# Rope queries of a latent-attention head in a zero-padded slot of 128 rows

## Chip, cores and metric

The kernel runs on one core of a Trainium2 chip, in one launch. The metric is the device time of the core in microseconds (us). Everything is float32: products that need accuracy split a float32 operand into a high part (`fp32r`, the form that TensorE takes in one pass) and a low part (the rest, again `fp32r`), and add three products: high by high, high by low, low by high.

## What is computed

Two layers over 256 latent tokens and 256 context tokens of width 2048. The first layer has eight heads of neighbourhood attention and eight heads of multi-head latent attention; the second is a bidirectional gated DeltaNet. The change is in the latent attention of the first layer. Cut to that:

```python
def mla_latent_attention(qn, qr, kn, kr, v, kn_c, kr_c, v_c):
    def attend(args):
        qn_i, qr_i = args
        s_lat = (einsum('bhqd,bhkd->bhqk', qn_i, kn) + einsum('bhqd,bkd->bhqk', qr_i, kr)) * MLA_SCALE
        s_ctx = (einsum('bhqd,bhkd->bhqk', qn_i, kn_c) + einsum('bhqd,bkd->bhqk', qr_i, kr_c)) * MLA_SCALE
        p_lat, p_ctx = joint_softmax(s_lat, s_ctx, v.dtype)
        return einsum('bhqk,bhkd->bhqd', p_lat, v) + einsum('bhqk,bhkd->bhqd', p_ctx, v_c)
```

A score is thus the sum of a product over the 128 plain dimensions of a head (`qn`, `kn`) and of a product over its 64 rope dimensions (`qr`, `kr`); the rope key `kr` is the same for all heads.

## The kernel before

Everything lies feature-major: a tile has 128 features on its partitions (rows) and 512 tokens along it, 256 latent then 256 context. TensorE takes the sum over the rows.

**Queues.** Each engine works through its own queue in order. A scheduler lays these queues out when the program is built, from its own estimates of how long things take, so an instruction that is added on one engine can move others, far behind it as well. Loads are issued by the SP queue.

**First layer, neighbourhood heads** (lines 395 to 404). `na_head` makes three tiles of 128x512 with 48 products each and `attend` (lines 350 to 388) does the attention. The last of them, head 7, is made at line 443 and attended at line 455, after the preparation of the latent heads.

**Preparation of the latent heads** (lines 408 to 460). `craw` holds the two normed low-rank inputs; lines 449 to 451 scale them and split them into `ch`, high by a cast on ScalarE (line 450), low by a subtraction on VectorE (line 451). `ch` takes the buffer that `hh` had, and `qr`, the rope queries, that of `hl`; both can be written only when the last product of head 7 has read `hh` and `hl`. Lines 457 to 460 make the rope queries: `qr` comes from four tiles, each the product of a 512-wide weight slice with `ch`, and each holds two heads, one in rows 0 to 63, the other in rows 64 to 127. `roped` (lines 427 to 439) scales a tile, rotates its latent half with a permutation product (`pp`, line 434) and three VectorE instructions, and calls `both`, which writes the high part (ScalarE) and the low part (VectorE) into `qr`. The rope key `kr` (line 441) holds its 64 rows twice, in rows 0 to 63 and in rows 64 to 127.

**The eight latent heads** (lines 461 to 470). Each loads its weights, makes `qT`, `kT` and `vT` with 12 products each (`dense`, lines 85 to 93) and calls `attend`. `attend` has four blocks of queries per head (two of latent tokens with 512 keys, two of context tokens with 256). For each block, `product` (lines 346 to 348) adds three products of `qT` with `kT` over 128 rows into the score tile `sp`, and line 368 three more of `qr` with `kr` over the 64 rows of the head:

```python
r = slice(64 * (h % 2), 64 * (h % 2) + 64)
attend(*o, 8 + h, None, ([qr[r, 4 * i + h // 2] for i in range(2)], [kr[r, i] for i in range(2)]))
```

Then come the maximum (line 372), the exponential (line 375), the division, four transposes (`pt`, line 381), the split into `PT` (`both`), and the products with the values (`po`, line 386). There are two score tiles, so a block's products can start when the block two before has been read by the exponential.

**Beside it** (`later`, `adaln`, lines 107 to 145). The modulation vectors of the second layer are made in the gaps: loads of 512 KB from `dn_wm` into three buffers `mraw`, four products `pmod` with 32 output rows on each (line 127), and per 16 loads a copy and four transposes. The three buffers lie in a pool that is opened when `craw` is released (line 453). `pmod` stands in TensorE's queue among the products of the heads.

After the latent heads come the output projection of the first layer (lines 477 to 503) and the second layer, whose first part has VectorE at work nearly all the time (solving the triangular systems, lines 759 to 782) and many switches of ScalarE's function tables (`ACT_TABLE_LOAD`).

Of the kernel before, what the change touches and what calls it, by code (L numbers as in the profile page):

```python
# [10 lines left out]
AF = mybir.ActivationFunctionType  # L11
# [7 lines left out]
T = 512  # L19
EPS = 1e-6  # L20
NA_SCALE = 128 ** -0.5
MLA_SCALE = 192 ** -0.5
# [4 lines left out]
def trunk_kernel(ctx: ExitStack, tc: tile.TileContext, g):  # L27
    nc = tc.nc
    V, A, PE, P = nc.vector, nc.scalar, nc.tensor, nc.gpsimd
# [8 lines left out]
    def mm_tile():  # L38
        return mmp.tile([128, T], F32, name="mm", tag="mm")
# [4 lines left out]
    def cst(name, shape, src=None):  # L44
        t = const.tile(shape, F32, name=name, tag=name)
        if src is not None:
            nc.scalar.dma_start(t, src)
        return t
# [3 lines left out]
    ones = cst("ones", [128, 128])  # L52
# [190 lines left out]
    with tc.tile_pool(name="s0", bufs=2) as tp, tc.tile_pool(name="s0p", bufs=1, space=PSUM) as ps:  # L243
# [37 lines left out]
        for j, (k0, n) in enumerate(GROUPS):  # L281
            ahead = mods_of(j + 1) if j < end else iter(())
            for i in range(0, NS, 2):
                own = i < NP
                p = [pz[i + e] if own else mm_tile() for e in range(2)]
# [16 lines left out]
    with tc.tile_pool(name="ab", bufs=2, reuse_waits="tile") as tp, \  # L302
# [4 lines left out]
        def later(pool, parts, after=None):  # L307
            for l, chunks, lanes in parts:
                if lanes:
                    yield from adaln_lanes(l, ps, "pm", pool, chunks, after)  # L310
                else:
                    yield from adaln(l, ps, ("pm", "pm"), pool, [(4 * ch, 4) for ch in chunks], after=after)
# [3 lines left out]
        def unit(xh, xl, src=None):  # L316
            nonlocal u, last_mm
            if src is None:
                src = wab[u]
                u += 1  # L320
            p = mm_tile()
            for c in range(0, 2048, 1024):
                last_mm = dense(p, load_split(src[:, c:c + 1024], 1024), 0, 8, xh, xl, k0=c // 128, first=c == 0, last=c > 0)
                steps(ahead, pace)
            return p

        for j in range(NS, KT):
            p = unit(hh, hl)
# [3 lines left out]
        def parts(src, name, n=T, scale=1.0, pool=None, bufs=1):  # L332

            t = (pool or tp).tile([128, 2, n], F32R, name=name, tag=name, bufs=bufs)
            both(t[:, 0], t[:, 1], src, scale)
            return t

        def both(hi, lo, src, scale=1.0):
            if scale == 1.0:
                A.copy(hi, src)  # L340
                V.tensor_tensor(lo, src, hi.bitcast(F32), op=ALU.subtract)
            else:
                A.mul(hi, src, scale)
                V.scalar_tensor_tensor(lo, src, scale, hi.bitcast(F32), op0=ALU.mult, op1=ALU.subtract)

        def product(ps, a, b, first, last):
            for i, (x, y) in enumerate(((0, 0), (0, 1), (1, 0))):
                PE.matmul(ps, a(x), b(y), start=first and i == 0, stop=last and i == 2)  # L348

        def attend(qT, kT, vT, h, bias=None, rope=None):  # L350

            pv = ps.tile([128, 4, 128], F32, name="pv", tag="tr", bufs=TR)
            for b in range(4):
                PE.transpose(pv[:, b], vT[:, b * 128:(b + 1) * 128], ident)
            vt = parts(pv.rearrange("p b d -> p (b d)"), "vt")
            po = ps.tile([128, T], F32, name="po", tag="st", bufs=1)
            for s in range(2):
                nk = 4 if s == 0 else 2
                c0 = 0 if s == 0 else S
                N = nk * 128  # L360
                PT = tp.tile([128, 2, 4, S], F32R, name="PT", tag="PT", bufs=1)
                for qb in range(2):
                    q0 = s * S + qb * 128
                    sp = ps.tile([128, T], F32, name="sp", tag="sp")
                    product(sp[:, :N], lambda i: qT[:, i, q0:q0 + 128], lambda i: kT[:, i, c0:T], True, rope is None)
                    if rope is not None:
                        qr, kr = rope
                        product(sp[:, :N], lambda i: qr[i][:, q0:q0 + 128], lambda i: kr[i][:, c0:T], False, True)
                    if s == 0 and bias is not None:
                        V.tensor_tensor(sp[:, :S], sp[:, :S], bias[:, qb], op=ALU.add)  # L370
                    mx = tp.tile([128, 1], F32, name="mx", tag="mx")
                    V.tensor_reduce(mx, sp[:, :N], axis=AX.X, op=ALU.max, negate=True)
                    pr = tp.tile([128, T], F32, name="pr", tag="pr")
                    sm = tp.tile([128, 1], F32, name="sm", tag="sm")
                    A.activation(pr[:, :N], sp[:, :N], AF.Exp, bias=mx, accum_out=sm)
                    rc = tp.tile([128, 1], F32, name="rc", tag="rc")
                    V.reciprocal(rc, sm)
                    V.tensor_scalar(pr[:, :N], pr[:, :N], rc, None, op0=ALU.mult)
                    pt = ps.tile([128, 4, 128], F32, name="pt", tag="tr", bufs=TR)
                    for b in range(nk):  # L380
                        PE.transpose(pt[:, b], pr[:, b * 128:(b + 1) * 128], ident)
                    qs = slice(qb * 128, (qb + 1) * 128)
                    both(PT[:, 0, :nk, qs], PT[:, 1, :nk, qs], pt[:, :nk])
                for b in range(nk):
                    c = (b if s == 0 else 2 + b) * 128
                    product(po[:, s * S:(s + 1) * S], lambda i: vt[:, i, c:c + 128], lambda i: PT[:, i, b],
                            b == 0, b == nk - 1)
                V.tensor_tensor(go[s][:, h], po[:, s * S:(s + 1) * S], go[s][:, h], op=ALU.mult)
# [6 lines left out]
        def na_head(h):  # L395
            bias = tp.tile([128, 2, S], F32, name="bias", tag="bias")
            nc.sync.dma_start(bias, g["rpb"][h])
            qT = parts(unit(hh, hl), "qT", scale=NA_SCALE)
            kT = parts(unit(hh, hl), "kT")
            vT = keep(unit(hh, hl), "vT")  # L400
            return qT, kT, vT, h, bias
# [20 lines left out]
        krp = unit(hh, hl)  # L422
# [1 line left out]
        nc.scalar.dma_start(rt, g["ropet"])  # L424
        cosT, sinT, perm = rt[:, :S], rt[:, S:2 * S], rt[:, 2 * S:]

        def roped(p, hi, lo, scale):
            out = tp.tile([128, T], F32, name="rope", tag="rope", bufs=1)
            if scale == 1.0:
                A.copy(out, p)  # L430
            else:
                A.mul(out, p, scale)
            pp = ps.tile([128, S], F32, name="pp", tag="tr", bufs=TR)
            PE.matmul(pp, perm, out[:, :S], start=True, stop=True)
            t = tp.tile([128, S], F32, name="rtmp", tag="mtmp")
            V.tensor_tensor(t, pp, sinT, op=ALU.mult)
            V.tensor_tensor(out[:, :S], out[:, :S], cosT, op=ALU.mult)
            V.tensor_tensor(out[:, :S], out[:, :S], t, op=ALU.add)
            both(hi, lo, out)

        kr = tp.tile([128, 2, T], F32R, name="kr", tag="kr", bufs=1)
        roped(krp, kr[:, 0], kr[:, 1], 1.0)
        na7 = na_head(7)
        ch = big.tile([128, KT, T], F32R, name="ch", tag="hh")
        qr = big.tile([128, KT, T], F32R, name="qr", tag="hl")
        for i, gain in enumerate((q_gain, kv_gain)):
            for k in range(4):
                j = 4 * i + k
# [3 lines left out]
        cr.release()  # L452
        mr = tc.alloc_tile_pool(name="mr2", bufs=2, reuse_waits="tile")
        ahead = later(mr, ((1, (2, 3, 8), 0),))
        attend(*na7)
        w = load_split(g["ab_wqr"])
        for j in range(4):
            p = mm_tile()
            dense(p, w, j * 512, 4, ch, ch[:, 8:])
            roped(p, qr[:, j], qr[:, 4 + j], MLA_SCALE)  # L460
        for h in range(8):
            w = load_split(g["ab_wb"][h], 1536)
            o = []
            for j, (k0, name, sc) in enumerate(((0, "qT", MLA_SCALE), (4, "kT", 1.0), (4, "vT", 1.0))):
                p = mm_tile()
                last_mm = dense(p, w, j * 512, 4, ch, ch[:, 8:], k0)
                o.append(keep(p, name) if name == "vT" else parts(p, name, scale=sc))
            r = slice(64 * (h % 2), 64 * (h % 2) + 64)
            steps(ahead, 1)
            attend(*o, 8 + h, None, ([qr[r, 4 * i + h // 2] for i in range(2)], [kr[r, i] for i in range(2)]))  # L470

        steps(ahead)
        steps(later(mr, ((1, (9,), 0),), last_mm))
# [10 lines left out]
        for j in range(KT):  # L484
# [3 lines left out]
            p = unit(gh, gl, g["ab_wo"][j])  # L488
# [127 lines left out]
    with tc.tile_pool(name="dn", bufs=2, reuse_waits="tile") as tp, \  # L616
# [14 lines left out]
        p = dunit(U_BA, FULL)  # L631
# [4 lines left out]
        hi = slice(64, 128)  # L636
# [22 lines left out]
        for d in range(2):  # L659
# [4 lines left out]
            for h in range(2):  # L664
                a = (d + h) % 2
                r = slice(64 * h, 64 * h + 64)
# [503 lines left out]
        for st in range(-2, 64 + LAG):  # L1170
            i, n = st // 4, st % 4
            j, m = (st - LAG) // 4, (st - LAG) % 4
# [85 lines left out]
        i = 0  # L1258
        for u in [v for e in range(KT - NE) for v in (e, NE + e)]:
            k0 = 24 if u < NE else 0  # L1260
            w = load_split(g["dn_wo"][u][:, 128 * k0:], 4096 - 128 * k0)
            p = (mm_tile() if i % 2 else ps.tile([128, T], F32, name="mm2", tag="ks"))[:, :S]
# [120 lines left out]
```

## Time and profile before

| | |
|---|---|
| median of 3 runs | 2562.46 us (2559.86 to 2563.72) |
| the profiled execution | 2556.45 us, of which 2554.6 us are the span from the first to the last instruction |
| mean granted TensorE clock | 0.984; 1.00 in all windows from 320 to 1068 us |
| busy: TensorE, weight loads, VectorE, ScalarE | 2461.1, 2004.0, 1849.1, 1130.7 us |
| latent heads | about 731 to 885 us of the span |
| preparation of the latent heads | about 640 to 731 us |
| second layer, VectorE part | about 1140 to 1760 us |

In the profile PE is TensorE's products, PEld its weight loads, DVE VectorE, ACT ScalarE, POOL GpSimd; SPq is SyncE's queue, which issues loads. A row of the timeline gives the start and the length in us, the line, the operation, output and input tiles, the part of the array that a product takes (rows * columns, 128*128 or 64*128 or 128*32), the size of the moving input, how many instructions of the kind follow one another, and in brackets the idle time of the engine before it with what ended it. A product's length overlaps with that of the next one, so the cost of a product in a row of products is read from start to start.

### The profile page before, as it was taken

To read this page: it belongs to the slowest core of one execution; us is meant where nothing else is said; L and a number is where in the kernel's file an instruction comes from. 1 tells how busy PE (TensorE), PEld (TensorE's weight loads), DVE (VectorE), ACT (ScalarE), POOL (GpSimd) and SP (SyncE) were. 2 spreads that over 40 slices of the span, in tenths; PEclk is the share of its full clock that TensorE was granted. 3 is DMA by queue.
4 is the path that set the end of the run, shared out by engine and by line. 5 is a ranking of instruction groups with operands and counts; after the bars stand their busy time and mean duration, and the time that the engine had idled before them with its cause. 6 is when DMAs were issued, how large, how long until landed. Compare 5 with 4: busy or idle time off the path is not lost.

```text
span 2554.6 us, 43393 instructions
## 1 busy us (share of the span) xinstructions
PE 2461.1 (96%) x16586; PEld 2004.0 (78%) x16586; DVE 1849.1 (72%) x3543; ACT 1130.7 (44%) x2454; POOL 275.4 (11%) x261
## 2 busy tenths in 40 slices
PE   6999999999999999989998999998999999999998
PEld 4657888888767688758888988887777777778898
DVE  4544788873445688758999999996677777777654
ACT  4223323332334422378656655643444445445453
POOL 0000000000000000023223332300000000003000
PEclk9999999999999999999999999998999999999999
DMA  8872655532343367644554545573233333335454
GB/s 259 289 254 87 201 167 165 184 118 94 100 155 119 109 212 228 219 138 150 167 158 156 161 153 162 162 223 95 88 105 112 113 100 107 112 92 180 151 189 139
DMA packets 201808, 394.30 MB, mean 154 GB/s; under 512 B 68224, under 2 KB 109696, under 8 KB 201472
## 3 DMA queue, kind: packets, MB, share of 16 engines
q1 hardware_dynamic: 200448, 389.98, 48.7%
q8 instruction: 131, 2.15, 0.4%
q10 hardware_dynamic: 1152, 1.54, 0.2%
q14 instruction: 77, 0.63, 0.1%
HBM read 356.28 MB, written 35.13 MB: 153 GB/s over the span
## 4 chain that ended last, share of the span: by engine, by line
PE 76%; DVE 11%; issue 6%; DMA 3%; ACT 3%; SPq 0%; POOL 0%; DVEq 0%; POOLq 0%; ACTq 0%
PE mm L90 19%; PE mm L91 18%; PE mm L92 18%; PE pks L988 3%; PE pmod L127 3%; DVE wlo L78 2%; PE sp L348 2%; PE ptr L1000 2%; DVE acc L561 2%; PE po L348 1%; DVE outer L773 1%; PE ptr L1033 1%; DVE L L759 1%; DVE X L775 1%; DVE U L782 1%
## 5 line engine op out<-in xcount | busy, mean ns | idle before, releaser
L90 PE MATMUL mm<-hh,whi 128*128 128x512 f32 (+1 forms) x2784 | 986.4, 355 | 2.7 <-ACT t L638 2.2
L92 PE MATMUL mm<-hh,wlo 128*128 128x512 f32 (+1 forms) x2784 | 957.9, 344 | 7.3 <-DVE wlo L78 6.7
L91 PE MATMUL mm<-hl,whi 128*128 128x512 f32 (+1 forms) x2784 | 960.3, 345 | 0.4 <-issue 0.4
L77 ACT CAST whi<-raw 128x1024 fp32r<-128x1024 f32 (+2 forms) x346 | 338.3, 982 | 651.5 <-PE mm L91 495.5
L90 PEld LDWEIGHTS mm<-hh,whi 128*128 128x128 f32 x2784 | 533.7, 192 | 113.1 <-issue 32.0
L92 PEld LDWEIGHTS mm<-hh,wlo 128*128 128x128 f32 x2784 | 533.4, 192 | 71.7 <-DVE wlo L78 8.0
L91 PEld LDWEIGHTS mm<-hl,whi 128*128 128x128 f32 x2784 | 534.1, 192 | 63.0 <-issue 10.3
L78 DVE TENSOR_TENSOR wlo<-raw,whi 128x1024 fp32r<-128x1024 f32 (+2 forms) x346 | 403.8, 1169 | 200.4 <-ACT whi L77 198.5
L163 DVE SCALAR_TENSOR_TENSOR lacc<-mraw,cond,lacc 128x512 f32<-128x512 f32 x300 | 208.0, 742 | 0.0
L561 DVE SCALAR_TENSOR_TENSOR acc<-cin,taps,acc 128x508 f32<-128x508 f32 (+3 forms) x256 | 193.9, 758 | 6.7 <-ACT acc L552 4.3
L1010 DVE SCALAR_TENSOR_TENSOR vl<-ptr,egm,vh 128x128 fp32r<-128x128 f32 x224 | 64.7, 346 | 99.8 <-ACT rf L1007 39.5
L715 POOL TENSOR_TENSOR rhs<-ghl,incl 128x512 fp32r<-128x512 f32 (+1 forms) x96 | 113.8, 1199 | 190.4 <-PE pd L717 171.0
L773 DVE SCALAR_TENSOR_TENSOR outer<-L,bv,X 128x31 f32<-128x31 f32 (+15 forms) x248 | 116.7, 471 | 5.5
L127 PE MATMUL pmod<-mraw,cond 128*32 128x512 f32 (+2 forms) x640 | 93.7, 500 | 25.4 <-DMA mraw<-ab_wm 18.0
L1094 DVE TENSOR_TENSOR wlo<-raw,whi 128x1024 fp32r<-128x1024 f32 x84 | 102.4, 1219 | 14.1 <-ACT whi L1086 14.0
L194 POOL TENSOR_TENSOR rs<-ms,half 128x4 f32<-128x4 f32 (+1 forms) x5 | 4.7, 947 | 984.7 <-DVE ms L192 984.7
L575 ACT ACTIVATE ac<-acc 128x128 f32<-128x128 f32 x160 | 37.6, 302 | 151.2 <-DVE acc L561 151.2
L775 DVE TENSOR_TENSOR X<-X,outer 128x31 f32<-128x31 f32 (+15 forms) x248 | 98.7, 398 | 4.7
L90 PE MATMUL mm<-gh,whi 128*128 128x512 f32 x256 | 99.9, 391 | 1.7 <-DVE x1B L493 1.7
L91 PE MATMUL mm<-gl,whi 128*128 128x512 f32 x256 | 99.9, 390 | 0.2 <-DVE gl L481 0.2
L92 PE MATMUL mm<-gh,wlo 128*128 128x512 f32 x256 | 99.7, 389 | 0.0
L1004 ACT ACTIVATE vh<-ptr,egm 128x128 fp32r<-128x128 f32 x224 | 71.7, 377 | 60.8 <-PE ptr L1000 54.4
(289 smaller groups left out, 3557.7 us busy)
## 6 DMA issues: line engine op xcount, KB each, us to landing
raw<-dn_w SPq DMA_DIRECT2D x194, 512.0 KB, 4.1
mraw<-dn_wm SPq DMA_DIRECT2D x96, 512.0 KB, 4.7
mraw<-ab_wm SPq DMA_DIRECT2D x88, 512.0 KB, 5.6
raw<-ab_w SPq DMA_DIRECT2D x66, 512.0 KB, 3.9
raw<-dn_wo SPq DMA_DIRECT2D x64, 512.0 KB, 3.7
raw<-ab_wo SPq DMA_DIRECT2D x32, 512.0 KB, 4.6
raw<-ab_w SPq DMA_DIRECT2D x32, 256.0 KB, 3.7
spt<-sp SPq DMA_DIRECT2D x64, 128.0 KB, 2.3
```

The lines of the kernel that those rows point to most:

```text
L77: A.copy(hi[:, :m], raw[:, :m])
L78: V.tensor_tensor(lo[:, :m], raw[:, :m], hi[:, :m].bitcast(F32), op=ALU.subtract)
L90: PE.matmul(ps, wh[:, c], xh[:, k0 + k, sl], start=first and k == 0, stop=False)
L91: PE.matmul(ps, wh[:, c], xl[:, k0 + k, sl], start=False, stop=False)
L92: end = PE.matmul(ps, wl[:, c], xh[:, k0 + k, sl], start=False, stop=last and k == kt - 1)
L127: PE.matmul(pmod[32 * q:32 * q + 32, :m], cond[:, 4 * kg + q, :], raw[c // 1024][:, half + c % 1024:half + c % 1024 + m], start=kg == 0, s ...
L163: V.scalar_tensor_tensor(acc[:, s], raw[:, q], cond[:, k, s:s + 1], acc[:, s], op0=ALU.mult, op1=ALU.add)
L561: V.scalar_tensor_tensor(o3[:, :, i0:i1], p3[:, :, i0 + d:i1 + d], taps[:, ch, t:t + 1], o3[:, :, i0:i1], op0=ALU.mult, op1=ALU.add)
L715: P.tensor_tensor(rhs, ghl[i].bitcast(F32)[:, d, kh * 8:kh * 8 + 2 * n].unsqueeze(2).broadcast_to(sh), incl[:, c].unsqueeze(1).broadcast_t ...
L773: V.scalar_tensor_tensor(o, L[:, rows, k:k + 1].broadcast_to([128, n, m]), bv[:, k:k + 1], X[:, k:k + 1, cols].broadcast_to([128, n, m]), ...
L775: V.tensor_tensor(X[:, rows, cols], X[:, rows, cols], o, op=ALU.subtract)
L1094: V.tensor_tensor(w, raws[j], h.bitcast(F32), op=ALU.subtract)
```

## The change

`qr` gets sixteen slots of 128 rows, two (high and low) for each of the eight heads. A head's 64 rope rows are written into its half of its own slot, the other 64 rows of the slot are filled with zeros by ScalarE (a copy of ones with scale 0), and the score product takes all 128 rows of `qr` and of `kr`, whose two halves are alike. `roped` writes a tile of two heads with two calls of `both`, of 64 rows each, where one of 128 rows was.

```diff
-        def roped(p, hi, lo, scale):
+        def roped(p, scale, parts_of):
...
-            both(hi, lo, out)
+            for r, hi, lo in parts_of:
+                both(hi, lo, out[r])
...
-        roped(krp, kr[:, 0], kr[:, 1], 1.0)
+        roped(krp, 1.0, [(slice(0, 128), kr[:, 0], kr[:, 1])])
...
+        rows = slice(0, 64), slice(64, 128)
...
-            roped(p, qr[:, j], qr[:, 4 + j], MLA_SCALE)
+            for e in range(2):
+                A.activation(qr[rows[1 - e], 4 * j + 2 * e:4 * j + 2 * e + 2],
+                             ones[rows[1 - e], 0:1].unsqueeze(2).broadcast_to([64, 2, T]), AF.Copy, scale=0.0)
+            roped(p, MLA_SCALE, [(rows[e], *[qr[rows[e], 4 * j + 2 * e + i] for i in range(2)]) for e in range(2)])
...
-            r = slice(64 * (h % 2), 64 * (h % 2) + 64)
...
-            attend(*o, 8 + h, None, ([qr[r, 4 * i + h // 2] for i in range(2)], [kr[r, i] for i in range(2)]))
+            attend(*o, 8 + h, None, ([qr[:, 2 * h + i] for i in range(2)], [kr[:, i] for i in range(2)]))
```

The number of products, their moving sizes and the arithmetic of a score stay; the zeros add nothing to a sum. Lines behind the change have numbers higher by 1 to 5 in the changed kernel.

## Prediction

> **What bounds the kernel now.** I read the page first: who is busy, and who ends the span.
>
> ```profile
> span 2554.6 us, 43393 instructions
> PE 2461.1 (96%) x16586; PEld 2004.0 (78%) x16586; DVE 1849.1 (72%) x3543; ACT 1130.7 (44%) x2454; POOL 275.4 (11%) x261
> PE 76%; DVE 11%; issue 6%; DMA 3%; ACT 3%; SPq 0%; POOL 0%; DVEq 0%; POOLq 0%; ACTq 0%
> ```
>
> PE is on the chain for 76% of the span. That is a mean over stages, so next come the windows: one in the neighbourhood heads, one in the preparation of the latent heads, one in those heads, and one in the second layer (the columns are the stage, its length, busy time and count of PE, PEld, DVE, ACT and POOL, then clock, DMA share and GB/s).
>
> ```profile
> 560.00:640.00 80.00, 80.00 (x385) 67.36 (x384) 27.93 (x40) 22.77 (x32) 1.01 (x1) 1.00 0.27 88
> 686.00:731.00 45.00, 39.90 (x193) 24.76 (x195) 25.77 (x54) 18.62 (x37) 0.00 (x0) 1.00 0.61 197
> 731.00:880.00 149.00, 147.91 (x768) 105.38 (x761) 80.81 (x174) 67.28 (x161) 0.00 (x0) 1.00 0.33 111
> 1400.00:1500.00 100.00, 93.03 (x1146) 86.25 (x1145) 97.53 (x152) 57.10 (x117) 31.85 (x32) 0.93 0.53 159
> ```
>
> In the latent heads PE idles 1.1 of 149 us at full clock, DVE and ACT work about half the time, and DMA is a third busy: PE sets the pace. In the preparation nobody is full (PE idles 5.1 of 45 us), so queues and waits set it. In the second layer's first part DVE is full.
>
> Now the score products themselves, from the row of their line, and one piece of the timeline of PE where two blocks of a latent head follow each other.
>
> ```profile
> L348 PE MATMUL sp<-kT,qT x192: 274/388/501, 299.9 to 882.1; 128*128 128x512 f32 x96, 128*128 128x256 f32 x96
> L348 PE MATMUL sp<-kr,qr x96: 272/388/502, 733.9 to 882.7; 64*128 64x512 f32 x48, 64*128 64x256 f32 x48
> ```
>
> ```profile
> 752.49 0.96 PE L348 MATMUL sp<-kr,qr 64*128 64x512 f32 x3
> 753.38 0.96 PE L348 MATMUL sp<-kT,qT 128*128 128x512 f32 x3
> 754.27 0.97 PE L348 MATMUL sp<-kr,qr 64*128 64x512 f32 x3
> 755.17 0.50 PE L90 MATMUL mm<-ch,whi 128*128 128x512 f32 x1
> 755.50 0.39 PE L91 MATMUL mm<-ch,whi 128*128 128x512 f32 x1
> 755.73 0.40 PE L92 MATMUL mm<-ch,wlo 128*128 128x512 f32 x1
> 755.97 0.39 PE L90 MATMUL mm<-ch,whi 128*128 128x512 f32 x1
> ```
>
> A product over 64 rows is as long as one over 128 (388 ns in the middle of both). From start to start a 512-wide product takes 0.23 us (755.50, 755.73). But the nine products from 752.49 to 755.17 take 2.68 us, where nine times 0.23 is 2.07: 0.61 more, 0.20 for each triple, and there is one edge between 64 and 128 rows to each triple. The first product behind an edge is the long one, 0.50 us, and its successor starts 0.33 behind it. The weight loads show what happens (one piece of the timeline with PE and PEld):
>
> ```profile
> 729.84 0.39 PE L90 MATMUL mm<-ch,whi 128*128 128x512 f32 x1
> 729.85 0.19 PEld L91 LDWEIGHTS mm<-ch,whi 128*128 128x128 f32 x1
> ...
> 733.92 0.53 PEld L348 LDWEIGHTS sp<-kr,qr 64*128 64x128 f32 x3 [0.37 <-issue]
> 734.81 0.30 PEld L348 LDWEIGHTS sp<-kT,qT 128*128 128x128 f32 x2 [0.36 <-issue]
> ```
>
> Among products of 128 rows the weights of L91 load while the product ahead of it, L90, runs. At an edge PEld idles 0.36 us for nothing that the profile shows.
>
> **What goes: the edges.** The 96 products over 64 rows stay 96, of the same width and, by the row above, the same length. PE's queue before holds them in 36 runs, which makes 72 edges. Two border on `pmod`, whose form 128*32 would make an edge with 128 rows too; they stay. Eight border on transposes; no row separates an edge there, so I count half. That leaves 66 edges at 0.20: 13.2 us. Bounds: the 32 blocks alone, 64 at 0.20, 12.8; all 72 at 0.21, 15.1. PE paces this stage, so this is time, less what a faster PE then waits for. The load waits of the preparation are the nearest row: 3.1 us in three waits. I take 1, for one more such wait, with bounds 0 and 3.
>
> ```profile
> PE pmod L127 <- DMA mraw<-dn_wm: 3.1, 3, 1.5
> ```
>
> **What comes: eight fills on ACT.** No row shows a fill of 64 rows by 1024. The nearest is the cast of 128x1024, 0.96 from its start to the next one's (686.30 to 687.26 below). Bounds: half of it, as half the rows are written, and 1.05; I take 0.96, since all rows work at once. What matters is where they stand. ACT's queue at the entry to the latent heads, where `ch` is the split input of all coming products (L464 is the fill; L451 is the old L450):
>
> ```order
>  L340 CAST kT<-mm 128x512
> -L77 CAST whi<-raw 128x1024 x2
> +L77 CAST whi<-raw 128x1024
> +L464 ACTIVATE qr<-ones 64x1024 x4
>  L392 COPY vT<-mm 128x512
> -L450 CAST ch<-craw 128x512 x8
> +L451 CAST ch<-craw 128x512 x8
> +L464 ACTIVATE qr<-ones 64x1024 x2
> +L375 ACTIVATE pr,sm<-sp,mx 128x512 x2
> +L464 ACTIVATE qr<-ones 64x1024
>  L340 CAST vt<-pv 128x512
> ```
>
> Four fills stand ahead of `vT` and `ch`, where one cast stood, and two more ahead of head 7's exponentials. Before, ACT, and below it PE, ran so:
>
> ```profile
> 686.30 1.06 ACT L77 CAST whi<-raw 128x1024 fp32r<-128x1024 f32 x1 [4.38 <-PE mm L91]
> 687.26 0.58 ACT L392 COPY vT<-mm 128x512 f32<-128x512 f32 x1
> 687.73 4.27 ACT L450 CAST ch<-craw 128x512 fp32r<-128x512 f32 x8
> ...
> 692.38 0.69 ACT L375 ACTIVATE pr<-sp,mx 128x512 f32<-128x512 f32 x1
> ```
>
> ```profile
> 690.35 0.50 PE L91 MATMUL mm<-ch,whi 128*128 128x512 f32 x1 [1.21 <-DVE ch L451]
> ...
> 695.46 0.88 PE L348 MATMUL sp<-kT,qT 128*128 128x256 f32 x6
> 696.17 0.40 PE L90 MATMUL mm<-ch,whi 128*128 128x512 f32 x1
> ...
> 698.92 1.03 PE L381 MATMUL pt<-ident,pr 128*128 128x128 f32 x8
> ...
> 703.49 1.05 PE L127 MATMUL pmod<-mraw,cond 128*32 128x512 f32 x4 [1.47 <-DMA mraw<-dn_wm]
> ```
>
> ```profile
> L451 DVE TENSOR_TENSOR ch<-craw,ch 128x512 fp32r<-128x512 f32 x8 | 5.0, 680 | 0.0
> L340 ACT CAST qr<-rope 128x512 fp32r<-128x512 f32 x4 | 2.5, 622 | 12.2 <-DVE rope L438 12.2
> ```
>
> The fills can start when the last product has read the old buffer, which is what ACT waited for at 686.30. Then `ch` starts at 686.30 + 4 x 0.96 + 0.47 (`vT`) = 690.6, not 687.73. PE's wait for the first low part ends at 690.6 + 0.53 (4.27 / 8) + 0.68 = 691.8, not 690.35: **1.4 us**. The exponentials come at 690.6 + 4.27 + 2 x 0.96 = 696.8, 4.4 later. The six products at 695.46 need the score tiles that these free, so PE waits there till about 697.5. Before, the twelve products of the next rope tile (696.17 to 698.92, 2.75 us) filled PE's time until the transposes `pt` were due. Now they stand behind them:
>
> ```order
>  L92 MATMUL mm<-ch,wlo 128x512
>  L348 MATMUL sp<-kT,qT 128x256 x6
> +L381 MATMUL pt<-ident,pr 128x128 x4
> +L127 MATMUL pmod<-mraw,cond 32x512 x4
> +L381 MATMUL pt<-ident,pr 128x128 x4
> +L127 MATMUL pmod<-mraw,cond 32x512 x2
>  L90 MATMUL mm<-ch,whi 128x512
>  L91 MATMUL mm<-ch,whi 128x512
> ```
>
> They also stand behind six `pmod`, whose third load PE awaited until 703.49 anyway. So the **2.75 us** are no longer under a wait: 4.2 us in all. Bounds: 1.4, if later load waits shrink by the rest, and 4.2 + 3.1 = 7.3, if all three come again in full.
>
> **The doubled `both`.** Four high casts and four low subtractions of 128 rows become eight and eight of 64 rows: at unchanged length 2.5 us more on ACT and 2.8 (4 x 0.69) on DVE. Their cover is ACT's idle time of 12.2 us ahead of these casts, in the second row above. Cost nothing; without the cover the rope tile, which has one buffer, would come 0.6 later four times, 2.5, which the upper bound of 7.3 holds. SP's queue is reordered there too: three `mraw` loads go ahead of one weight load that is due a head later; nothing.
>
> **The second layer.** No line of it is changed, but its order is. The piece that I price is ACT's queue where the decays (`neg`, `egm`, `eglb`) and the first silu tiles (`ac`) are made, first before, then now:
>
> ```order
> 519 L572 ACT_TABLE_LOAD
> 520 L572 ACTIVATE ac_9159<-acc 128x128 x2
> 521 L667 ACT_TABLE_LOAD
> 522 L667 ACTIVATE neg<-pg 64x128
> 523 L668 ACTIVATE egm<-pg 64x128
> 524 L669 ACTIVATE eglb<-pg 128x128
> 525 L667 ACTIVATE neg<-pg 64x128
> 526 L668 ACTIVATE egm<-pg 64x128
> 527 L669 ACTIVATE eglb<-pg 128x128
> 528 L572 ACT_TABLE_LOAD
> 529 L572 ACTIVATE ac_9159<-acc 128x128 x2
> 530 L575 ACTIVATE ac_9243<-acc 128x128
> ```
>
> ```order
> 524 L577 ACT_TABLE_LOAD
> 525 L577 ACTIVATE ac_9175<-acc 128x128 x4
> 526 L77 CAST whi<-raw 128x1024
> 527 L580 ACTIVATE ac_9259<-acc 128x128 x2
> 528 L672 ACT_TABLE_LOAD
> 529 L672 ACTIVATE neg<-pg 64x128
> 530 L673 ACTIVATE egm<-pg 64x128
> 531 L674 ACTIVATE eglb<-pg 128x128
> ```
>
> ```profile
> 1140.13 1.28 ACT L572 ACT_TABLE_LOAD   x1
> ...
> 1152.39 1.28 ACT L720 ACT_TABLE_LOAD   x1
> ```
>
> ```profile
> DVE neg L670 <- ACT neg L667: 7.9, 1, 7.9
> PE px L793 <- DVE U L782: 18.8, 8, 5.7
> ```
>
> These two rows are the first and the last of four such loads, which stand no more between the first silu and the first decay product: 4 x 1.28 = 5.1 us less on ACT, for which DVE waits there (7.9). Six more stand later in the queue (70 in all, 68 before), where ACT is busy 57 of 100 us. I take 2 us of gain; bounds 5.1 of gain, and 6 x 1.28 = 7.7 of loss if all six are met by a waiting DVE.
>
> **Sum:** -13.2 + 1 + 4.2 - 2 = -10.0 us. The profiled execution took 2556.45 us, its span of 2554.6 and 1.85 around it; it would take 2546.45. The median of the runs is 6 us above that execution, so against 2562.46 I forecast 2552.5.
>
> **Rivals.** About 0.2%, 5.1 us, is what a measurement of this kernel can tell from no change.
>
> *PE stops being the pace of the latent heads.* Each head's softmax chain and buffers stay as long, and PE's work shrinks by 9% (13.2 of 149). For: 1.1 us of waits are there already, and the loads into three buffers go at PE's pace. Against: DVE and ACT have half their time free, and in the neighbourhood heads with the same `attend` PE idles 0 of 80 us. If half of the gain goes into waits: -6.6 + 4.2 - 2 = -4.4, 2558.1. Chance 0.18.
>
> *The edges don't go*, the change doing nothing where it aims, because the load that waits isn't waiting for the change of rows. Then 0 + 4.2 - 2 = +2.2, 2564.7. The Trainium skill (TensorE: Matmul & The Clock Gate, section on what overlaps and what doesn't) says that a weight load overlaps running products only when its row group differs; by that rule 128-row loads would wait just as the 64-row ones do, and this would be the outcome. The fence with PEld speaks against it: L91's load runs inside L90's product on the same 128 rows. Chance 0.05.
>
> *Slower: the second layer starves DVE.* At three places in PE's queue some fifteen 256-wide products moved from ahead of `px` to behind it, and PE waits at `px` for DVE 18.8 us in eight waits already, the longest 5.7. If all eight became 5.7, that is 26.8 more; with half of it reaching DVE, 13.4, and the 7.7 of table loads, 21.1 is lost against -8.0 without the 2: +13.1, 2575.6. It decides from 13.1 lost on. Against it: DVE is full there (97.53 of 100), and what it does is no more than before. Chance 0.06.
>
> **How the numbers follow.** The forecast has 0.71: 2552.5, its own range -17 to -5, from edges of 12.8 to 15.1, an entry of 1.4 to 7.3 and a second layer of -5.1 to some +3. All of it is faster by over 5.1 but the last tenth of a us. The first two rivals are within 0.2%: 0.18 + 0.05 = 0.23. The third is slower: 0.06. The range of 8 in 10 takes the forecast's own and most of the first rival, -17.5 to -0.5: 2545 to 2562.
>
> **What would show it.** In the profile after: no 64*128 form; the rows of `sp<-kr,qr` at 0.23 from start to start, with PEld no longer idle ahead of them; the latent heads some 12 us shorter; the first `ch` low part near 692 and the preparation some 4 longer; ACT's fills at 0.96. Wrong would be: PE waits in the latent heads of over 5 us, an edge of 0.20 where none should be, or a second layer that moves by more than 5.

## The result, and the profile after

The changed kernel took 2546.07 us in the median of its runs (2542.68 to 2553.14), the kernel before 2562.76 us beside it: a ratio of 0.9939, 95% interval 0.9928 to 0.995. That is 16.7 us less, more than the 10 that was forecast and near the end of the range of 2545 to 2562; two further sets of runs on other chips gave 20.1 and 12.9 us less (below). The profiled execution after took 2550.65 us, 4.6 above the median of its runs; the profiled execution before lay 6 below the median of its own.

First the page's head and the shares of the chain of waits. PE is busy 12.5 us less than before with as many products, and is still the pace.

```profile
span 2548.9 us, 43398 instructions
PE 2448.6 (96%) x16586; PEld 2002.5 (79%) x16586; DVE 1853.5 (73%) x3547; ACT 1140.4 (45%) x2468; POOL 275.6 (11%) x261
PE 74%; DVE 12%; issue 6%; DMA 4%; ACT 3%; POOL 0%; SPq 0%; DVEq 0%; POOLq 0%; ACTq 0%
```

The windows of the preparation, and of the latent heads from their first rope score product to the last (columns as before). In the heads PE idles 1.3 us of 135.0. In the preparation the granted clock, 1.00 before, is 0.96, and ACT works 7.7 us more in this stretch.

```profile
686.00:731.00 45.00, 39.12 (x180) 23.04 (x178) 25.34 (x51) 26.29 (x44) 0.00 (x0) 0.96 0.55 186
...
741.97:877.00 135.03, 133.71 (x761) 106.12 (x759) 80.18 (x177) 67.75 (x164) 0.00 (x0) 1.00 0.36 117
```

The rows of the score products' line, and the timeline of PE and PEld in the first block of a latent head. The form 64*128 is gone. The weights of the rope products load while the products ahead of them run, with no bracket of idle time, and a triple takes 0.69 us (741.97 to 742.66), where it took 0.89.

```profile
L348 PE MATMUL sp<-kT,qT x192: 274/386/499, 301.9 to 876.6; 128*128 128x512 f32 x96, 128*128 128x256 f32 x96
...
L348 PE MATMUL sp<-kr,qr x96: 278/376/398, 742.0 to 876.9; 128*128 128x512 f32 x48, 128*128 128x256 f32 x48
```

```profile
741.27 0.86 PE L348 MATMUL sp<-kT,qT 128*128 128x512 f32 x3
741.51 0.19 PEld L348 LDWEIGHTS sp<-kT,qT 128*128 128x128 f32 x1
741.74 0.65 PEld L348 LDWEIGHTS sp<-kr,qr 128*128 128x128 f32 x3
741.97 0.85 PE L348 MATMUL sp<-kr,qr 128*128 128x512 f32 x3
742.43 0.42 PEld L348 LDWEIGHTS sp<-kT,qT 128*128 128x128 f32 x2
742.66 0.63 PE L348 MATMUL sp<-kT,qT 128*128 128x512 f32 x2
```

The entry to the latent heads, on ACT and then on PE. Four fills take 1.04 us each (688.32 to 692.48; forecast 0.96), and PE now waits 3.23 us for `vT`, where it waited 1.21 for the first low part of `ch`. What nothing in the forecast had: the ten products behind that wait (693.62 to 697.80) start 0.43 us apart, not 0.23. The window over them shows why: the granted clock is 0.57. The six products at 701.00 wait for nothing.

```profile
688.32 4.26 ACT L464 ACTIVATE qr<-ones 64x1024 fp32r<-64x1024 f32 x4 [4.38 <-PE mm L91]
692.48 0.56 ACT L392 COPY vT<-mm 128x512 f32<-128x512 f32 x1
692.95 4.26 ACT L451 CAST ch<-craw 128x512 fp32r<-128x512 f32 x8
```

```profile
693.10 0.65 PE L354 MATMUL pv<-ident,vT 128*128 128x128 f32 x4 [3.23 <-ACT vT L392]
693.62 0.73 PE L90 MATMUL mm<-ch,whi 128*128 128x512 f32 x2
694.34 0.79 PE L91 MATMUL mm<-ch,whi 128*128 128x512 f32 x1
...
696.64 0.63 PE L90 MATMUL mm<-ch,whi 128*128 128x512 f32 x1
697.07 0.63 PE L91 MATMUL mm<-ch,whi 128*128 128x512 f32 x1
697.49 0.47 PE L92 MATMUL mm<-ch,wlo 128*128 128x512 f32 x1
697.80 0.39 PE L90 MATMUL mm<-ch,whi 128*128 128x512 f32 x1
698.03 0.39 PE L91 MATMUL mm<-ch,whi 128*128 128x512 f32 x1
...
701.00 0.88 PE L348 MATMUL sp<-kT,qT 128*128 128x256 f32 x6
```

```profile
694.00:698.00 4.00, 4.00 (x11) 2.93 (x10) 4.00 (x8) 3.98 (x8) 0.00 (x0) 0.57 0.00 0
```

And the groups of ACT's rope casts and of the decay product, with the waits at `px`. The doubled casts have 15.3 us of idle time ahead of them. VectorE waits 3.2 us for `neg`, where it waited 7.9, and PE waits 7.9 us at `px`, where it waited 18.8.

```profile
L340 ACT CAST qr<-rope 64x512 fp32r<-64x512 f32 x8 | 4.9, 618 | 15.4 <-DVE rope L438 15.3
...
L675 DVE TENSOR_SCALAR neg<-neg 128x256 f32<-128x256 f32 x1 | 0.3, 295 | 3.2 <-ACT neg L672 3.2
```

```profile
PE px L798 <- DVE U L787: 7.9, 6, 2.7
```

To compare stages, each profile is cut at the same instructions: A the first `pp`, B the first and C the last rope score product, D the last `x1A`, E the first and F the last transpose `L`. A to B is the preparation from the rope key on (called the entry), B to C the latent heads, D to E the start of the second layer, E to F its VectorE part. Lengths in us, from the starts in the rows of each tile; the kernels are described below.

| profile | 0-A | A-B | B-C | C-D | D-E | E-F |
|---|---|---|---|---|---|---|
| before | 657.5 | 76.4 | 148.8 | 186.5 | 113.4 | 511.9 |
| before, second profile | 659.1 | 76.9 | 151.0 | 188.2 | 112.8 | 513.0 |
| changed | 659.5 | 82.5 | 134.9 | 188.3 | 107.1 | 517.5 |
| changed, two more | 660.1, 658.4 | 81.4, 82.6 | 135.0, 134.9 | 188.3, 186.6 | 107.1, 107.1 | 516.2, 517.8 |
| 64 rows in the slots | 659.2 | 82.9 | 147.2 | 186.5 | 108.4 | 517.5 |
| padded keys, by GpSimd | 659.5 | 80.9 | 135.4 | 186.7 | 111.9 | 517.2 |
| padded keys, by ScalarE | 659.5 | 77.6 | 135.4 | 188.3 | 113.4 | 512.7 |
| plain and rope in turn | 659.1 | 74.4 | 174.9 | 186.5 | 106.0 | 515.1 |
| fills by GpSimd | 658.9 | 80.4 | 136.0 | 188.3 | 108.8 | 513.5 |
| fills late | 659.1 | 80.3 | 135.7 | 188.3 | 110.6 | 513.9 |
| decays together | 658.6 | 76.2 | 148.6 | 186.5 | 105.6 | 517.6 |
| both, two profiles | 658.7, 659.8 | 77.3, 77.9 | 135.4, 135.4 | 186.7, 186.7 | 106.3, 105.4 | 512.7, 515.3 |

### The profile page after: what moved, and what is told of

Read it like the earlier page. It is cut to its first block, busy times and chain, and to the rows that moved or that the text cites. A ratio compares the mean times of both kernels' runs of the same rounds, so it can differ in the third digit from the quotient of the medians.

```text
span 2548.9 us, 43398 instructions
## 1 busy us (share of the span) xinstructions
PE 2448.6 (96%) x16586; PEld 2002.5 (79%) x16586; DVE 1853.5 (73%) x3547; ACT 1140.4 (45%) x2468; POOL 275.6 (11%) x261
## 4 chain that ended last, share of the span: by engine, by line
PE 74%; DVE 12%; issue 6%; DMA 4%; ACT 3%; POOL 0%; SPq 0%; DVEq 0%; POOLq 0%; ACTq 0%
PE mm L90 19%; PE mm L91 17%; PE mm L92 17%; PE pks L993 3%; PE pmod L127 3%; DVE wlo L78 3%; PE ptr L1005 2%; DVE acc L566 2%; PE sp L348 2%; DVE outer L778 1%; PE po L348 1%; DVE X L780 1%; DMA mraw<-dn_wm 1%; DVE U L787 1%; PE ptr L1038 1%
## 5 line engine op out<-in xcount | busy, mean ns | idle before, releaser
L92 PE MATMUL mm<-hh,wlo 128*128 128x512 f32 (+1 forms) x2784 | 959.3, 345 | 12.2 <-DVE wlo L78 11.5
L720 POOL TENSOR_TENSOR rhs<-ghl,incl 128x512 fp32r<-128x512 f32 (+1 forms) x96 | 113.1, 1193 | 186.6 <-PE pd L722 165.9
L1099 DVE TENSOR_TENSOR wlo<-raw,whi 128x1024 fp32r<-128x1024 f32 x84 | 102.5, 1220 | 14.0 <-ACT whi L1091 13.4
```

What stands on the lines that cost most here:

```text
L92: end = PE.matmul(ps, wl[:, c], xh[:, k0 + k, sl], start=False, stop=last and k == kt - 1)
L720: P.tensor_tensor(rhs, ghl[i].bitcast(F32)[:, d, kh * 8:kh * 8 + 2 * n].unsqueeze(2).broadcast_to(sh), incl[:, c].unsqueeze(1).broadcast_t ...
L1099: V.tensor_tensor(w, raws[j], h.bitcast(F32), op=ALU.subtract)
```

## Experiments

The theory after the result (1): the edges between 64- and 128-row products are worth some 13 us, and the new order of the rest is a gain too, from the start of the second layer, less a loss at the entry. One rival (2): the edges give nothing and all comes from the order. Another (3): the order gives nothing and the edges all of it. Four kernels told these apart on one chip, the changed kernel among them:

> The changed kernel once more, as the control of this set. Both theories: about 16 us below the kernel before (ratio near 0.994). Its profile gives a second execution, so that a stage that differs between the two profiles of the same kernel is not taken for an effect of the change.

Measured: 2545.06 us beside 2565.16 for the kernel before, ratio 0.993 (0.9917 to 0.9943), 20.1 less.

**64 rows in the slots:** the changed kernel, with its fills and its queues, but each product takes the head's 64 rows alone, so the edges are back.

```diff
-            attend(*o, 8 + h, None, ([qr[:, 2 * h + i] for i in range(2)], [kr[:, i] for i in range(2)]))
+            attend(*o, 8 + h, None, ([qr[rows[h % 2], 2 * h + i] for i in range(2)], [kr[rows[h % 2], i] for i in range(2)]))
```

> Everything of the change is kept (sixteen slots, fills, doubled splits, and by the built queues the very order of the changed kernel on every engine), but each score product takes the head's 64 rows of its slot again. Theory 1 (the edges are worth about 13 us, the new order and the fills together -16.7 + 13 = about -4): 13 us slower than the changed kernel, 4 us faster than the one before. Theory 2 (the gain comes from the order that the scheduler happens to make, the edges are hidden behind waits): equal to the changed kernel, 16 us faster than before. Theory 3 (all of the gain is edges, and entry and second layer cancel): equal to before within 3 us.

Measured: 2560.08 us, ratio 0.9987 (0.9978 to 0.9996). The edges cost 15.0 us by the medians (2560.08 - 2545.06) and 12.2 us in the latent heads (147.2 to 135.0). The order with the fills gains 5.1 by the medians without them; the interval of the ratio allows 1.0 to 5.6.

**Padded keys:** the other way about. Queries packed as before, and two copies of the rope keys with one half zero, written by GpSimd into free slots of the `qr` tile; the queues of PE, ACT, DVE and SP are those of the kernel before.

```diff
+        for e in range(2):
+            P.tensor_scalar(qr[rows[1 - e], 8 + 2 * e:10 + 2 * e],
+                            ones[rows[1 - e], 0:1].unsqueeze(2).broadcast_to([64, 2, T]), 0.0, None, op0=ALU.mult)
+            P.tensor_copy(qr[rows[e], 8 + 2 * e:10 + 2 * e], kr[rows[e]])
...
-            attend(*o, 8 + h, None, ([qr[r, 4 * i + h // 2] for i in range(2)], [kr[r, i] for i in range(2)]))
+            attend(*o, 8 + h, None, ([qr[:, 4 * i + h // 2] for i in range(2)], [qr[:, 8 + 2 * (h % 2) + i] for i in range(2)]))
```

> The kernel before with its queues of TensorE, VectorE, ScalarE and SyncE unchanged in order; all score products take 128 rows, because instead of the queries the keys are padded: GpSimd, idle there, writes two copies of the rope keys with zeros in the other half. No fills on ScalarE, no doubled splits, no new order. Theory 1: the edges alone, 12 to 15 us faster than before, so 2 to 4 us slower than the changed kernel. Theory 2: within 3 us of before. Theory 3: 16 us faster than before. The latent heads should be 13 us shorter in its profile and the preparation as long as before.

Measured: 2552.22 us, ratio 0.995 (0.9936 to 0.9964), 12.9 less; latent heads 135.4. So the edges go in the old order too, and by as much, and the rival that gave all to the order falls. The one that gave it nothing is only weakened: the changed kernel is 7.2 us faster than this one, but the two intervals just overlap, and in the next set the padded keys and the changed kernel came out equal. The entry took 80.9 all the same, 4.0 to 4.5 more than before, though no queue but GpSimd's has changed. The groups of 686 to 712 us show `ch`'s eight low parts at 958 ns each, where they took 680, beside GpSimd's fills and copies:

```profile
L456 DVE TENSOR_TENSOR ch<-craw,ch 128x512 fp32r<-128x512 f32 x8 | 7.2, 958 | 0.0
L448 POOL TENSOR_SCALAR qr<-ones 64x1024 fp32r<-64x1024 f32 x2 | 6.0, 2987 | 37.4 <-PE mm L91 37.4
...
L450 POOL CAST qr<-kr 64x1024 fp32r<-64x1024 f32 x2 | 2.5, 1251 | 0.1
```

That alone is a small part: PE's wait for the first low part grows by 0.56 us only (1.77 for 1.21). Most of the rest is TensorE's clock, which is near half of full speed behind this wait and again behind one of 2.13 us for a load at 716.88; the two windows lose 1.7 and 1.6 us, where the kernel before had 1.00.

```profile
694.00:698.00 4.00, 4.00 (x12) 3.08 (x11) 4.00 (x6) 1.91 (x5) 2.93 (x2) 0.57 0.00 0
718.00:722.00 4.00, 4.00 (x11) 3.23 (x12) 1.87 (x4) 0.62 (x1) 0.00 (x0) 0.59 0.41 131
```

**Fills by GpSimd:** the changed kernel with its eight fills as `P.tensor_scalar(..., 0.0, None, op0=ALU.mult)` in place of `A.activation(..., AF.Copy, scale=0.0)`.

> The changed kernel with its eight fills on GpSimd instead of ScalarE; the scheduler makes another order from it. Theory 1 with an entry cost of 4 to 6 us by the fills: the preparation shorter by 3 to 6 us in the profile; the total 3 to 6 us below the changed kernel, if the second layer's order does not undo it. If the fills cost nothing at the entry: the preparation as long as in the changed kernel.

Measured: 2549.9 us, ratio 0.9945 (0.9932 to 0.9957). That is 4.8 us above the changed kernel beside it, so no gain over ScalarE, and the expectation failed. The entry falls to 80.4 only; here too `ch`'s low parts are slow (911 ns each), PE waits 1.79 us for the first, and the clock behind it is below full speed again (0.81 and 0.76 from 690 to 698 us).

The next set, on another chip, took the second layer and the entry apart.

**Decays together:** the kernel before, with one thing changed in the second layer: the first head's silu tiles stand behind the twelve decay exponentials on ACT.

```diff
-                A.activation(eglb[:, a, h], pg[:, 2 + h], AF.Exp)
+                decays = A.activation(eglb[:, a, h], pg[:, 2 + h], AF.Exp).ins
...
-        tile_act(ac2, acc, AF.Silu, halves)
+        with tc.issue_after(behind) if behind else nullcontext():
+            tile_act(ac2, acc, AF.Silu, halves)
...
-            acq = conv_of(pq, kh, False)
+            acq = conv_of(pq, kh, False, decays if kh == 0 else None)
```

> The kernel before, untouched up to the second layer; there the first head's silu tiles on ScalarE are queued behind all twelve decay exponentials, so that two table loads instead of six stand between the first of them and the first decay product, as in the changed kernel (which has another order in many places besides). Theory A (the order at the start of the second layer is a gain of its own, four table loads of 1.28 us that VectorE waits for): the stretch from the last x1A to the first transpose L shrinks by 4 to 6 us from 113.4 / 111.9, VectorE's wait for neg falls from 7.9 to about 3, and the time falls by 4 to 6 us against the kernel before. Theory B (the lead is used up in the next stretch, where VectorE and the loads have their own pace, and what the changed order gained came from elsewhere): the stretch shrinks, the time moves by less than 2 us.

Measured: 2558.52 us beside 2561.83, ratio 0.9985 (0.9976 to 0.9994), 3.3 less. The time lies between the two theories. The start of the second layer falls from 113 to 105.6 us, by more than expected, and VectorE's wait for `neg` is gone:

```profile
L671 DVE TENSOR_SCALAR neg<-neg 128x256 f32<-128x256 f32 x1 | 0.3, 288 | 0.0
```

The order of those exponentials is thus a gain of its own. How much of the 7 us stays is less sure: this profile's E to F took 517.6 (at a granted clock of 0.95), and the interval of the time allows 1.5 to 6.1.

**Padded keys by ScalarE:** as above, but the four instructions are ACT's, each pair queued behind the scaling of the second or third rope tile.

```diff
+            with tc.issue_after(scaled[e + 1]):
+                A.activation(qr[rows[1 - e], 8 + 2 * e:10 + 2 * e],
+                             ones[rows[1 - e], 0:1].unsqueeze(2).broadcast_to([64, 2, T]), AF.Copy, scale=0.0)
+                A.copy(qr[rows[e], 8 + 2 * e:10 + 2 * e], kr[rows[e]])
```

> The padded keys again, written by ScalarE and not by GpSimd, in its idle time ahead of the second and third rope casts; queues of all engines are those of the kernel before, but for these four instructions. Theory A (edges are worth 13 in the latent heads, and the entry costs only where ch is held up): the latent heads take 135 us, the entry stays at the 76 to 78 us of the kernel before and not at the 81 of the changed kernel, the time falls by 13 to 16 us against the kernel before (2 to 5 better than the padded keys on GpSimd). Theory C (the preparation's end is set by loads whenever the stage is disturbed): the entry takes 80 again, and the time falls by 10 to 12.

Measured: 2548.6 us, ratio 0.9951 (0.9939 to 0.9963), 13.2 less; entry 77.6, heads 135.4. This is nearly the edges' gain alone, with neither the fills ahead of `ch` nor the order. The changed kernel took 2548.92 us beside it (below), so there the rest of its change was worth nothing in sum.

**Both of these:**

> Both of these together: padded keys by ScalarE, silu tiles behind the decays; nothing of the changed kernel's fills for queries. If the parts add up (theory A): 13 to 16 plus 4 to 6, so 17 to 22 us below the kernel before and 0 to 5 below the changed kernel. If the second layer's lead is used up (theory B): 12 to 16 below the kernel before.

> The changed kernel beside these on the same chip, to rank them: 17 to 20 us below the kernel before, as in the two sets of runs so far, whatever the theory.

Measured: both together 2541.15 us, ratio 0.9918 (0.9905 to 0.9932), 20.7 less; the changed kernel beside them 2548.92 us, ratio 0.9955 (0.9942 to 0.9967), 12.9 less, which misses the expected 17 to 20. So in this set this version beats both kernels. It was run once more, on another chip and without the changed kernel beside it:

> The padded keys with the silu tiles behind the decays a second time, to see whether its 20.7 us below the kernel before stand. If the two parts add up as they came alone (13.2 and 3.3): 16.5 below; if the first reading holds: 18 to 23 below. Either way its interval should lie below that of the padded keys alone (0.9939 to 0.9963). Stages: entry 77, latent heads 135, stretch ahead of the first L 106.

Measured: 2545.68 us beside 2563.18, ratio 0.993 (0.9917 to 0.9944), 17.5 less: the parts (13.2 and 3.3) about add up. Its interval just overlaps that of the keys alone, which was not expected, and the 17.5 lies among the 12.9 to 20.1 of the changed kernel, so its lead over that kernel rests on the one set.

The last set: a second look at the kernel before, more edges, and the fills moved.

> The kernel before, for a second profile of it, since the first one was of an execution below all its timed runs. If that execution was a short one by chance (the part from the first to the last transpose L took 512 us at a clock of 0.96 there, 517 us at 0.95 in other kernels of the same order), the profile now has some 517 in that part or some 1 to 2 us more in the part ahead of the preparation; the entry (76.4), the latent heads (148.8) and the stretch ahead of the first L (113.4) come again within 1.5 us. If those three differ, the stage lengths read so far can't carry a term of this size.

Measured: 2562.13 us beside 2562.4; the profiled span is 2563.1 us, 8.5 above the first profile's. The entry and the start of the second layer came again within 0.6 us, the latent heads only within 2.2, where 1.5 was set. So one profile gives the length of the latent heads to some 2 us, and no better.

**Plain and rope in turn:** the kernel before, its six products per block alternating, so that its queue has 192 edges where it had 72.

```diff
-                    product(sp[:, :N], lambda i: qT[:, i, q0:q0 + 128], lambda i: kT[:, i, c0:T], True, rope is None)
...
-                        product(sp[:, :N], lambda i: qr[i][:, q0:q0 + 128], lambda i: kr[i][:, c0:T], False, True)
+                        for i, (x, y) in enumerate(((0, 0), (0, 1), (1, 0))):
+                            PE.matmul(sp[:, :N], qT[:, x, q0:q0 + 128], kT[:, y, c0:T], start=i == 0, stop=False)
+                            PE.matmul(sp[:, :N], qr[x][:, q0:q0 + 128], kr[y][:, c0:T], start=False, stop=i == 2)
```

> The kernel before with the six products of a block in turn, plain, rope, plain, rope, plain, rope, so that its PE queue has 96 runs of 64-row products and 192 edges, where it had 36 and 72; nothing else is edited (the scheduler's order of the rest comes near to that of the changed kernel). Theory A (an edge costs 0.20 us because the weights behind it aren't loaded ahead): 120 more edges, 24 us, so the latent heads go from 148.8 to about 173 us and the time to 15 to 24 us above the kernel before (with the gain of the other order). Rival (what the changed kernel gains in the latent heads is not tied to the edges but to having fewer half-height products at all): the same 96 products, the same 148 us.

Measured: 2580.11 us, ratio 1.0074 (1.0055 to 1.0093), 17.7 more. The latent heads took 174.9 us, so 120 more edges cost 23.9 to 26.1 us (from 151.0 and 148.8): 0.20 to 0.22 each, or 0.01 less if the two `pmod` products that moved into the heads, some 0.9 us, are taken off. The rival of the same 148 us falls. Its timeline of PE shows every product now 0.43 behind the last one at a granted clock of 1.00 (ten steps from 755.88 to 760.16 in 4.28 us):

```profile
755.88 0.49 PE L371 MATMUL sp<-kr,qr 64*128 64x512 f32 x1
756.30 0.50 PE L370 MATMUL sp<-kT,qT 128*128 128x512 f32 x1
756.74 0.50 PE L371 MATMUL sp<-kr,qr 64*128 64x512 f32 x1
...
760.16 0.50 PE L371 MATMUL sp<-kr,qr 64*128 64x512 f32 x1
760.59 0.50 PE L90 MATMUL mm<-ch,whi 128*128 128x512 f32 x1
760.93 0.40 PE L91 MATMUL mm<-ch,whi 128*128 128x512 f32 x1
```

```profile
733.45:908.30 174.85, 172.62 (x776) 112.06 (x775) 82.76 (x177) 68.52 (x164) 0.00 (x0) 1.00 0.30 99
```

**Fills late:** the changed kernel, its fills in ACT's idle time behind the scaling of the second and third rope tile.

```diff
+            with tc.issue_after(scaled[1 + j // 2]):
+                for e in range(2):
+                    A.activation(qr[rows[1 - e], 4 * j + 2 * e:4 * j + 2 * e + 2],
+                                 ones[rows[1 - e], 0:1].unsqueeze(2).broadcast_to([64, 2, T]), AF.Copy, scale=0.0)
```

> The changed kernel with its eight fills queued behind the scaling of the second and third rope tile on ScalarE, where it idles, and so no longer ahead of vT, ch and head 7's exponentials (the decays stand together, as in the changed kernel). Theory A (the entry's 5 to 6 us come from where the fills stand, not from the fills): entry 77 to 79 us, latent heads 135, stretch ahead of the first L 105 to 107; 3 to 6 us below the changed kernel, 18 to 23 below the kernel before. Rival (the entry is set by loads that come late however the fills stand, as the run with fills on GpSimd suggests, 80.4): 81 to 83 us again, the time within 2 us of the changed kernel.

Measured: 2552.72 us, ratio 0.9961 (0.9949 to 0.9974), so no better than the changed kernel, and the expected time failed. At the entry, `ch` is on time again (its wait is back at 1.21) and the clock stays at 1.00. The entry still takes 80.3, 3.4 to 3.9 more than before. Some 1.75 of that is no loss, four `pmod` products that moved there from the heads (explained below); the rest goes with the waits at `pmod`, which have grown to 5.0 us in four, from 3.1 and 3.5 in the two profiles of before. So where the fills stand did matter at the entry; the time was lost elsewhere, some 3.5 us of it at the start of the second layer (110.6 for 107.1, at a granted clock of 0.92 for 0.94 to 0.97). The two rows of PE's waits from 684 to 742 us:

```profile
PE pmod L127 <- DMA mraw<-dn_wm: 5.0, 4, 1.9
PE mm L91 <- DVE ch L454: 1.2, 1, 1.2
```

## Why the prediction was right, and where not

**The edges** (13.2) were right in size and in cause. Counted in several ways they are 12.2 us (64 rows in the slots), 13.4 (padded keys in the old order, against the first profile of before; 15.6 against the second) and about 0.20 apiece when they are multiplied. The Trainium skill (TensorEngine Tiling (Array Packing), Key Properties of the tiling modes) says that a change of the tiling mode drains TensorE; the traces agree in that each change here costs about 0.20 us, but they don't show by themselves that a drain is what fills this time. The rival that the edges stay fell, and the rule that it went by does not hold here: the rope products' 128-row weights load inside the products ahead of them on the same rows (741.74 within 741.27).

**One microsecond for waits of a faster PE** was not needed: PE idles 1.3 us in the latent heads, 1.1 before. The rival that PE stops being the pace falls with it.

**The entry** (4.2) came out near its size by luck; here a step failed. A to B is 5.6 to 6.1 us longer (4.5 to 6.2 over the three profiles of the changed kernel). Of this, 2.0 is the first wait (3.23 for 1.21; forecast 1.4, with fills of 0.96 for 1.04). Some 1.7 is the half clock behind it (4 us at 0.57). And some 1.75 is no loss: PE's queue has 32 `pmod` products between the first product with `ch` and the first rope score product, where it had 28, and 32 in the heads, where it had 36. (A load of `mraw` serves two of these products, not four as the description of the kernel has it, and a copy follows 8 loads, not 16.) Each leaves two rows in the trace, and eight rows take 1.80 us in the same stage of the padded keys by ScalarE:

```profile
701.88 1.80 PE L127 MATMUL pmod<-mraw,cond 128*32 128x512 f32 x8
```

So the latent heads' 13.9 us (148.8 to 134.9) contain that 1.75, and the loss at the entry is 3.9 to 4.4. The step that failed is "So the 2.75 us are no longer under a wait": the waits for `mraw` were 3.2 us, as before, and PE did not wait for the exponentials at 701.00, since at half clock it came there later itself. A loss by the clock, which the forecast did not have, stands in for a loss that did not come.

**The doubled `both`** cost nothing, as forecast: ACT has 15.3 us of idle time ahead of it.

**The second layer** (-2) held as a sum, though both of its parts were larger than the sum lets see. Its start fell by 5.7 to 6.3 us, the bound of 5.1 (all four table loads met by a waiting VectorE) and a little more; 11 loads stand there, where 15 did, and the kernel with the decays together shows the cause alone. The six loads that the forecast saw further on then stand in the VectorE part: 57 from E to F in the changed kernel, 51 before. With 51 and a granted clock of 0.96 this part took 511.9 to 513.5 us (five profiles, among them both of before); with 57 and the same clock 515.1 to 517.5 (three). So some 3.5 us are given back there, of a bound of 7.7; this is a comparison of profiles, not an experiment on these loads alone. D to F as a whole is 623.3 to 624.9 us in the three profiles of the changed kernel, 625.3 and 625.8 before: 0.4 to 2.5 less. The sign of being wrong, a second layer that moves by over 5, showed in its start and not in its sum. The kernel with the decays together kept 51 loads there, and so did the one with the padded keys beside it, whose D to F is 619.0 and 620.7. The slower rival fell: the waits at `px` shrank from 18.8 to 7.9 us.

The rows of E to F, before and after, show the added work on ScalarE (311.19 to 317.24 us) at the same clock:

```profile
1182.60:1694.50 511.90, 483.44 (x4895) 443.14 (x4894) 493.95 (x819) 311.19 (x604) 144.42 (x142) 0.96 0.54 165
```

```profile
1172.30:1689.80 517.50, 478.19 (x4867) 438.02 (x4866) 494.25 (x817) 317.24 (x609) 142.54 (x142) 0.96 0.53 162
```

**The base.** From the second profile of before to the profile after, the stages give +0.4 + 5.6 - 16.1 + 0.1 - 5.7 + 4.5 and -3.0 behind F: 14.2 us less. From the first profile it is 5.8, because that execution was 6 us below the median, as the forecast said without asking where, and the one after 4.6 above its own. Three sets of runs gave 16.7, 20.1 and 12.9, so the excess over the forecast of 10 is 3 to 10 us. The missing waits explain 1 of it. For the rest no one stage shows more than some 1 us in all three profiles of the changed kernel, and one profile gives a stage to some 2 us only, so its cause stays open. Beside the padded keys, which have the edges' gain without the new order, the changed kernel was 7.2 us faster in one set and equal in another: what its order is worth in sum is not settled.

## What to carry to other kernels

Between products of 64 and of 128 rows the weights were not loaded ahead here, and each change cost about 0.20 us, nearly as much as a 512-wide product (0.23); where 64-row operands stand among 128-row ones, pad one side with zeros, and choose the side that has fewer copies and can be written when its engine idles (two padded keys did what sixteen slots of queries did). Look at what else a new order has moved before you credit the edit, and follow it to the end of the stage behind: here the table loads of a layer that nobody touched gave some 6 us at its start and cost some 3.5 later, and a few lines of their own had the gain without the later loads (3.3 us by the medians). Profile the kernel before twice when a few us matter.

## What the runs showed of the hardware

**The clock of TensorE halves behind some short waits.** All four profiles with the fills ahead of `vT` have some 4 us at about half clock behind the 3.23 us wait (0.50 to 0.75 in windows of 2 us). Both profiles of before have 1.00 all through that stage. It is not the length of the wait alone: the padded keys by ScalarE lost it behind 1.74 us, as the first row shows and, in its window, the clock of 0.63 (those by GpSimd behind 1.77 and 2.13), while the fills late kept it through a wait of 1.86.

```profile
705.73 1.05 PE L127 MATMUL pmod<-mraw,cond 128*32 128x512 f32 x4 [1.74 <-DMA mraw<-dn_wm]
706.71 0.44 PE L381 MATMUL pt<-ident,pr 128*128 128x128 f32 x2
706.90 2.60 PE L348 MATMUL po<-PT,vt 128*128 128x256 f32 x11
```

```profile
706.00:710.00 4.00, 4.00 (x21) 2.96 (x19) 0.46 (x2) 0.41 (x2) 0.00 (x0) 0.63 0.77 259
```

The Trainium skill (TensorE: Matmul & The Clock Gate, section The HAM clock gate) has the array fall to half rate after an idle window of about 3.4 us and come back after as much work. The half rate and the length of the slow stretch agree (0.43 for 0.23 us, some 4 us); all the waits here, 1.74 to 3.23 us, are shorter than such a window, so a whole idle window was not needed. Here it makes a wait of 3 us cost 5, and it may be part of why equal stages differ by some us between runs, which no run here shows.

**GpSimd slows VectorE.** Beside its fills and copies the subtractions of `ch` took 911 to 958 ns each, alone 680; they read two tensors each. Work was moved to an idle engine, and the busy one paid, though PE's wait for them grew by 0.6 us only.

**Writing half the rows saved ScalarE nothing.** The casts of 64x512 took 618 ns, those of 128x512 622; a fill of 64x1024 took 1055 ns, about a cast of 128x1024 (1040).
